# RWKV-7 and band attention on one core: the inverse's products on 64x64 tiles, head sums as float32 products

## The chip, the cores and the metric

The kernel runs on one core of a Trainium2 chip. A core has TensorE (matrix products; in the profile PE for the products and PEld for the loads of their stationary, left operand), VectorE (DVE), ScalarE (ACT), GpSimd (POOL) and SyncE (SP), which work side by side and wait for each other through semaphores; transfers run on 16 DMA engines. SBUF holds operands in 128 partitions, PSUM takes the products. The metric is the time of one execution on the device, in microseconds.

## The reference, cut to what matters

Two layers over 256 tokens of width 2048: first an RWKV-7 layer (time mixing and an MLP), then a layer of chunked band attention (and an MLP), with adaLN modulation everywhere. The change lies in the time mixing, a recurrence over tokens for each of 32 heads of width 64:

```python
def step(S, inp):
    r_t, w_t, k_t, v_t, kk_t, a_t = inp
    sa = jnp.einsum('bhvk,bhk->bhv', S, -kk_t)
    S = (S * w_t[:, :, None, :] + sa[..., None] * (kk_t * a_t)[:, :, None, :]
         + v_t[..., None] * k_t[:, :, None, :])
    y = jnp.einsum('bhvk,bhk->bhv', S, r_t)
    return S, y
```

Three sums over the 64 elements of a head stand around it: the squared length of `kk`, by which `kk` is divided; the sum of `r*k*r_k`, which is multiplied by `v` and added to `y`; and the variance of `y` in the group norm.

## The kernel before, in words

Activations lie transposed: channels in partitions, the 256 tokens along the free side. The 2048 channels are 16 blocks of 128 partitions, and a block holds two heads of 64: a "pair". The large products use a split of each float32 operand into a rounded part and a remainder (`halves`, `split`), and take three single-pass products in two instructions (`proj2`, L394 and L395, tiles `pj`).

The recurrence is computed in chunks of 64 tokens, four chunks for a head. Within a chunk it needs the inverse of a 64x64 unit triangular matrix I + A, where A comes from the products `gr` of L97. `Pair.invert` builds it by doubling: the inverse of the diagonal blocks of size 1 is known; level l joins blocks of 2^l to blocks of 2^(l+1) by two products, with the part of A that couples them (`al`: A times a 0/-1 mask) as left operand of the first. Up to level 4 everything stays inside the two diagonal 32x32 blocks of a head's 64x64 matrix. Level 5 joins those two blocks by the corner block.

In the kernel before, the two diagonal blocks of the two heads of a pair lie under each other: `da` is 128 partitions x 4 chunks x 32, a 32-partition strip (`QS`) per block. The corner blocks lie in `co`. `Pair.tiles` (L103) makes a level's product as 16 small products of 32x32 on four diagonal tiles of TensorE. A level is: a transpose of `u` by VectorE (`tt`, L235), a mask by GpSimd (`al`, L239), a product into `iv`, a copy by ScalarE (`xs`, L241), a second product, an addition by VectorE (L252). Level 0 needs no product (L222, L224). Level 5 works with the strips crosswise, and GpSimd and VectorE put the 64x64 inverse together in `uf` (L247, L256).

A head sum (`head_sums`, L120) is a product with a 128x128 matrix of ones in each head's block (`bones`). It takes single-pass products: `parts` (L110 to L115) lets ScalarE write the rounded values `sH`, and GpSimd the remainder `sL`, and the product is taken of both.

What sets the order: `layer_a` (stages at its end) runs the pairs as a pipeline. In round p, TensorE has the projections of pair p (`proj_steps`, the "dense" work), `early` of pair p-1 (lora products, decay, normalised operands, two head sums), `invert` of pair p-2 and `late` of pair p-3 (the chain over the four chunks, tiles `chn` and `py`, and the third head sum). A round has 16 slots; in each slot `late`, `invert` and `early` advance by their share of steps (a step ends at a `yield`), and then the dense work, held behind the last product of the small work of the slot before. In the last three rounds the first output projections (`out_steps`, L383 to L385, tiles `o`) are the dense work. Within these edges the framework's planner sets the order on each engine. The weights and the adaLN matrix (`acc`, L423) stream in on SyncE's queue all the time.

Of the kernel before, what the change touches and what calls it, by code (L numbers as in the profile page):

```python
# [36 lines left out]
def _constants():  # L37
    i = np.arange(C)
    parts, at = [], {}

    def put(name, a):
        a = np.asarray(a, np.float32)
        if a.shape[0] == C:
            a = np.concatenate([a, a], 0)
        at[name] = (sum(p.shape[1] for p in parts), a.shape[1])
        parts.append(a)

    put("cols", np.tile(np.array([RMS_EPS, GN_EPS, -0.5, 1.0, 1 / 32], np.float32), (P, 1)))
# [12 lines left out]
    p = np.arange(P)  # L61
    bones = (p[:, None] // C == p[None, :] // C).astype(np.float32)
# [7 lines left out]
QS = [slice(H * i, H * i + H) for i in range(4)]  # L70
C_RMS, C_GN, C_MHALF, C_ONE, C_32ND = range(5)


class Pair:
# [15 lines left out]
    @staticmethod  # L90
    def ch(t):
        return t.rearrange("p (c t) -> p c t", t=C)

    def each(self, o, lhsT, rhs):
        for c in range(4):
            for K in self.heads:
                self.b.nc.tensor.matmul(o(c)[K], lhsT(c)[K], rhs(c)[K], start=True, stop=True)  # L97

    def tiles(self, o, lhsT, rhs, pairs):

        for c in range(4):
            for R, K in pairs:
                self.b.nc.tensor.matmul(o[QS[K], c, :], lhsT[QS[R], c, :], rhs[QS[R], c, :], start=True, stop=True,  # L103
                                        tile_position=(H * R, H * K))

    def parts(self, func, src, scale=1.0):

        nc, pw = self.b.nc, self.b.pw
        H, L = (pw.tile([P, T], F32R, tag=n, bufs=2, name=n) for n in ("sH", "sL"))
        nc.scalar.activation(H, src, func, scale=scale)  # L110
        if func != AF.Copy:
            t = self.s("pt", 2)
            nc.scalar.activation(t, src, func, scale=scale)
            src = t
        nc.gpsimd.tensor_tensor(out=L, in0=src, in1=H, op=ALU.subtract)  # L115
        return H, L

    def head_sums(self, ps, parts):
        for i, t in enumerate(parts):
            self.b.nc.tensor.matmul(ps, self.b.bones, t, start=(i == 0), stop=(i == 1))  # L120

    def early(self):
# [7 lines left out]
        nc.tensor.matmul(z[:, 0:T], lw[:, 0, :], self.tw, start=True, stop=True)  # L130
        nc.tensor.matmul(z[:, T:2 * T], lw[:, 1, :], self.ta, start=True, stop=True)
# [7 lines left out]
        sq = self.parts(AF.Square, k, vec("k_k", j))  # L139
# [39 lines left out]
        rkp = self.parts(AF.Copy, rkp)  # L179
# [13 lines left out]
    def invert(self):  # L193
        b, nc, s, ch, kr, bk, bh, kh = self.b, self.b.nc, self.s, self.ch, self.kr, self.bk, self.bh, self.kh
        cst, pp = b.cst, b.pp

        def every(name):
            return cst(name).unsqueeze(1).to_broadcast([P, 4, H])

        def half(name, bufs):  # L200
            return b.pw.tile([P, 4, H], F32, tag=name, bufs=bufs, name=name)

# [28 lines left out]
        uf = self.u = b.uf[self.j % 2]  # L231
        down, up = ((0, 1), (2, 3)), ((1, 0), (3, 2))
        for l in range(1, 6):
            tt_, xs = half("tt", 1), half("xs", 1)
            nc.vector.transpose(out=tt_.rearrange("p c t -> p (c t)"), in_=u.rearrange("p c t -> p (c t)"))  # L235
            pi = pp.tile([P, 16, H], F32, tag="iv", bufs=1, name="iv")[:, 0:4, :]
            if l < 5:
                al = half("al", 2)
                nc.gpsimd.tensor_tensor(out=al, in0=da, in1=every(f"lev{l}"), op=ALU.mult)  # L239
                self.tiles(pi, al, tt_, [(i, i) for i in range(4)])  # L240
                nc.scalar.copy(xs, pi)  # L241
            else:
                self.tiles(pi, co, tt_, down)
                for i, K in enumerate(QS):
                    if i % 2:
                        nc.scalar.copy(xs[K], pi[K])
                    nc.gpsimd.tensor_copy(uf[K, :, H * (i % 2):H * (i % 2) + H], u[K])  # L247
            yield
            pi = pp.tile([P, 16, H], F32, tag="iv", bufs=1, name="iv")[:, 0:4, :]
# [12 lines left out]
            yield  # L262

    def late(self):
# [7 lines left out]
        for c in range(4):  # L272
            pch = pp.tile([P, 3, C], F32, tag="chn", bufs=1, name="chn")
            g, sa = (pw.tile([P, C], F32, tag=n_, bufs=2, name=n_) for n_ in ("g", "sa"))
            for K in heads:
                nc.tensor.matmul(pch[K, 0, :], mk[K, c, 0:C], bk[K, 2, c, :], start=True, stop=(c == 0))  # L276
            if c:
                for K in heads:
                    nc.tensor.matmul(pch[K, 0, :], kr[K, c, 0:C], zs[K, :], start=False, stop=True)
            nc.scalar.copy(g, pch[:, 0, :])  # L280
            yield
            for K in heads:
                nc.tensor.matmul(pch[K, 1, :], u[K, c, :], g[K, :], start=True, stop=True)
            nc.scalar.mul(sa, pch[:, 1, :], -1.0)
            for K in heads:
                nc.tensor.matmul(ch(py)[K, c, :], bk[K, 2, c, :], mk[K, c, C:P], start=True, stop=False)
            if c:
                for K in heads:
                    nc.tensor.matmul(ch(py)[K, c, :], zs[K, :], kr[K, c, C:P], start=False, stop=False)
            yield  # L290
            if c < 3:
                for K in heads:
                    nc.tensor.matmul(pch[K, 2, :], bk[K, 1, c, :], bk[K, 2, c, :], start=True, stop=False)
                for K in heads:
                    nc.tensor.matmul(pch[K, 2, :], bk[K, 0, c, :], sa[K, :], start=False, stop=True)
# [7 lines left out]
            for K in heads:  # L303
                nc.tensor.matmul(ch(py)[K, c, :], sa[K, :], ch(ar)[K, c, :], start=False, stop=True)
# [3 lines left out]
        sq = self.parts(AF.Square, py)  # L308
# [8 lines left out]
        for i in range(2):  # L317
            nc.tensor.matmul(pg, self.lg[:, i, :], self.tg[:, i, :], start=(i == 0), stop=(i == 1))
# [5 lines left out]
class Body:  # L324
# [8 lines left out]
    def cst(self, name, rows=slice(None)):  # L333
        o, n = CST_AT[name]
        return self.csts[rows, o:o + n]
# [184 lines left out]
    def run(self):  # L520
# [16 lines left out]
        self.lazy, self.fins = False, iter(())  # L537
        self.ada_done = set()
# [40 lines left out]
    def layer_a(self, st, sp):  # L579
# [169 lines left out]
        with ExitStack() as s1:  # L749
# [5 lines left out]
            self.bones = pw.tile([P, P], F32R, name="bones")  # L755
            self.uf = [pw.tile([P, 4, C], F32, name=f"uf_{i}") for i in range(2)]
            nc.scalar.copy(self.bones, self.cst("bones"))
            for e, u in zip(e01, self.uf):
                nc.vector.memset(e[:, :, 0:1], 1.0)
                nc.gpsimd.memset(u, 0.0)  # L760
# [39 lines left out]
            stages = ((Pair.late, 16), (Pair.invert, 13), (Pair.early, Pair.EARLY), (None, 16))  # L800
# [290 lines left out]
```

## Time and profile before

| | |
|---|---|
| runs of the kernel before, us | 2772.35, 2776.08, 2783.49 (median 2776.08) |
| the profiled execution's own time, us | 2773.6 |
| its span, us | 2771.8 |
| mean granted TensorE clock | 0.986 |
| 32x32 product instructions (L103) | 4608, from 256.5 to 735.4 us |

The span is the time from the first to the last instruction that the profiler recorded. Each group of instructions has its line in the kernel, the tiles it writes and reads (`out<-in`), its shape (for products the rows and columns of TensorE that it uses, then the moving operand), a count, busy time and mean duration. Matmuls overlap, so the distance between starts says more than a duration. "A <- B" says that A waited for B.

### The profile page before, as it was taken

The numbers are of one execution on the slowest core, as the hardware profiler recorded it, in microseconds if no ns is written. First come the engines' busy times: TensorE is split into PE (matmuls) and PEld (weight loads), VectorE is DVE, ScalarE is ACT, GpSimd is POOL, SyncE is SP. The second block draws the span as 40 slices with busy tenths as digits, with TensorE's granted clock in tenths as the row PEclk, the third lists the DMA queues.
The fourth block names the chain that finished last, engine by engine and source line by source line (L and its number), as shares of the span: only waits on it lengthen the run. The fifth ranks groups of instructions, "written<-read, shape, count | busy, mean of one in ns | idle before, by whom it ended". The sixth has DMA issues, their size and how long they took to land.

```text
span 2771.8 us, 57644 instructions
## 1 busy us (share of the span) xinstructions
PE 2653.9 (96%) x23402; PEld 2217.6 (80%) x23402; DVE 2087.3 (75%) x3098; ACT 1260.9 (45%) x2214; POOL 301.8 (11%) x416
## 2 busy tenths in 40 slices
PE   6998999999998999999999899999989999999997
PEld 3677777777887888888888788877878888888886
DVE  4568778878889888888788896799786566665665
ACT  2345555556344434344344354465444344443444
POOL 0003443443220000000000200000100000000002
PEclk9999999999999999999999999999999999999999
DMA  9886556555687888888888868888876555555553
GB/s 297 269 281 193 169 171 196 176 176 162 216 302 243 298 308 305 300 314 296 299 306 302 304 218 282 268 293 268 279 242 216 187 186 186 187 183 189 185 188 122
DMA packets 217387, 662.60 MB, mean 239 GB/s; under 512 B 21408, under 2 KB 68896, under 8 KB 217120
## 3 DMA queue, kind: packets, MB, share of 16 engines
q1 hardware_dynamic: 215056, 656.36, 71.5%
q8 instruction: 184, 3.01, 0.4%
q10 hardware_dynamic: 2064, 2.54, 0.3%
q14 instruction: 83, 0.68, 0.1%
HBM read 656.72 MB, written 2.10 MB: 238 GB/s over the span
## 4 chain that ended last, share of the span: by engine, by line
PE 76%; DVE 9%; DMA 7%; issue 4%; POOL 1%; ACT 1%; DVEq 0%; SPq 0%; ACTq 0%; POOLq 0%
PE pj L394 40%; PE pj L395 20%; DMA raw<-w_ada 5%; DVE wL L363 3%; DVE acc L423 2%; PE iv L103 2%; PE gr L97 1%; DMA raw<-w_ada_kv 1%; PE m L625 1%; DVE un L504 1%; PE o L383 1%; PE ms L97 1%; POOL sL L115 1%; PE chn L276 1%; DVE aHL L506 1%
## 5 line engine op out<-in xcount | busy, mean ns | idle before, releaser
L394 PE MATMUL pj<-aHL,wH 128*128 128x512 f32 x3712 | 1353.5, 405 | 26.0 <-DVE aHL L506 22.4
L360 ACT CAST wH<-raw 128x1024 fp32r<-128x1024 f32 x772 | 807.0, 1047 | 949.4 <-PE pj L394 622.1
L363 DVE TENSOR_TENSOR wL<-raw,wH 128x1024 fp32r<-128x1024 f32 x772 | 946.1, 1228 | 290.7 <-ACT wH L360 288.8
L395 PE MATMUL pj<-aHL,wL 128*128 128x256 f32 x3712 | 1049.3, 283 | 7.5 <-DVE wL L363 7.2
L394 PEld LDWEIGHTS pj<-aHL,wH 128*128 128x128 f32 x3712 | 700.3, 189 | 199.2 <-issue 28.0
L394 PE MATMUL pj<-hHL,wH 128*128 128x512 f32 x2048 | 722.0, 397 | 4.5 <-DVE hHL L882 4.5
L395 PEld LDWEIGHTS pj<-aHL,wL 128*128 128x128 f32 x3712 | 705.3, 190 | 14.6 <-DVE wL L363 11.9
L395 PE MATMUL pj<-hHL,wL 128*128 128x256 f32 x2048 | 574.3, 281 | 4.6 <-DVE wL L363 4.5
L423 DVE SCALAR_TENSOR_TENSOR acc<-raw,ct,acc 128x1024 f32<-128x1024 f32 x360 | 470.4, 1307 | 139.8 <-DMA raw<-w_ada 104.0
L394 PEld LDWEIGHTS pj<-hHL,wH 128*128 128x128 f32 x2048 | 384.3, 188 | 97.9 <-DVE hHL L882 6.7
L395 PEld LDWEIGHTS pj<-hHL,wL 128*128 128x128 f32 x2048 | 386.8, 189 | 8.1 <-DVE wL L363 7.7
L482 POOL TENSOR_TENSOR ss<-ss,sq 128x256 f32<-128x256 f32 x56 | 65.0, 1160 | 1599.7 <-ACT sq L481 1599.4
L901 DVE SCALAR_TENSOR_TENSOR x<-pj,mod,x 128x256 f32<-128x256 f32 x256 | 123.1, 481 | 51.7 <-PE pj L395 48.8
L881 ACT CAST hHL<-t 128x256 fp32r<-128x256 f32 x128 | 51.4, 403 | 67.6 <-DVE t L880 67.3
L625 PE MATMUL m<-rawa,crep 128*32 128x256 f32 x512 | 47.4, 449 | 17.5 <-DMA rawa<-w_ada 16.9
L481 ACT ACTIVATE sq<-x 128x256 f32<-128x256 f32 x60 | 25.0, 418 | 70.5 <-DVE x L901 39.6
L880 DVE SCALAR_TENSOR_TENSOR t<-t 128x256 f32<-128x256 f32 x128 | 53.9, 422 | 3.0
L882 DVE TENSOR_TENSOR hHL<-t,hHL 128x256 fp32r<-128x256 f32 x128 | 53.4, 418 | 0.6 <-ACT hHL L881 0.5
L862 DVE TENSOR_TENSOR t<-pj,t 128x256 f32<-128x256 f32 x128 | 53.2, 417 | 0.0
L239 POOL TENSOR_TENSOR al<-da,csts 128x128 f32<-128x128 f32 x64 | 40.7, 647 | 67.4 <-PE iv L103 62.7
L861 ACT COPY t<-pj 128x256 f32<-128x256 f32 x128 | 46.6, 366 | 0.0
L685 PE MATMUL t<-aHL,wH 128*128 128x256 f32 x128 | 38.1, 298 | 5.8 <-DVE v L693 3.6
(230 smaller groups left out, 2483.0 us busy)
## 6 DMA issues: line engine op xcount, KB each, us to landing
raw<-w_ada SPq DMA_DIRECT2D x320, 512.0 KB, 4.7
raw<-w_up SPq DMA_DIRECT2D x256, 512.0 KB, 4.9
raw<-w_down SPq DMA_DIRECT2D x256, 512.0 KB, 4.3
rawa<-w_ada SPq DMA_DIRECT2D x64, 512.0 KB, 6.8
raw<-w_ada_kv SPq DMA_DIRECT2D x64, 512.0 KB, 5.4
raw<-w_k SPq DMA_DIRECT2D x32, 512.0 KB, 4.2
raw<-w_r SPq DMA_DIRECT2D x32, 512.0 KB, 4.7
raw<-w_o SPq DMA_DIRECT2D x32, 512.0 KB, 5.2
```

The source lines that it names most:

```text
L97: self.b.nc.tensor.matmul(o(c)[K], lhsT(c)[K], rhs(c)[K], start=True, stop=True)
L103: self.b.nc.tensor.matmul(o[QS[K], c, :], lhsT[QS[R], c, :], rhs[QS[R], c, :], start=True, stop=True, tile_position=(H * R, H * K))
L360: nc.scalar.copy(Hf, raw)
L363: eng.tensor_tensor(out=Lf, in0=raw, in1=Hf, op=ALU.subtract)
L394: nc.tensor.matmul(ps, H[:, i, :], a(kt), start=(kt == 0), stop=False)
L395: ins = nc.tensor.matmul(ps[:, 0, :], L[:, i, :], a(kt)[:, 0, :], start=False, stop=(kt == KT - 1))
L423: nc.vector.scalar_tensor_tensor(out=acc, in0=raw, scalar=ck, in1=acc, op0=ALU.mult, op1=ALU.add)
L482: (eng or nc.gpsimd).tensor_tensor(out=self.ss, in0=self.ss, in1=sq, op=ALU.add)
L625: nc.tensor.matmul(ps[g:g + 32, part, :W], crep[:, kt, :], raw[:, i, :], start=(part == 1 and kt < 4), stop=(part == 0 and kt >= KT - 4), ...
L880: nc.vector.scalar_tensor_tensor(out=t, in0=t, scalar=0.0, in1=t, op0=ALU.max, op1=ALU.mult)
L882: nc.vector.tensor_tensor(out=h[:, 1, :], in0=t, in1=h[:, 0, :], op=ALU.subtract)
L901: nc.vector.scalar_tensor_tensor(out=x, in0=ps[:, i, :], scalar=self.mods[(layer, 5)][:, n:n + 1], in1=x, op0=ALU.mult, op1=ALU.add)
```

## The change

The diagonal blocks are not taken out of A any more: `A` is a copy of the whole 64x64 matrices (128 partitions x 4 chunks x 64), and the level masks are 64 columns wide. A product of the inverse is made by `each` (L97's form): eight products of 64x64, one per chunk and head, whose moving operand `tt` or `u` has 32 columns (a head's two diagonal blocks under each other). For this the left operand must be 64x64 with zeros off the two blocks: the mask sees to it in the first product of a level; for the second, ScalarE copies the first product twice, once with the even strips kept and the odd ones zeroed, once the other way round (`spread`, with the new constant columns `C_EVEN`, `C_ODD`). Level 0 is now a product of its own with the identity, followed by an addition and a transpose. Level 5 uses two tiles that are zeroed once (`corner`), of which only one half is written. `uf` comes from a ring of two tiles.

A head sum is now two float32 products of 64x64 form (one per head, ones as left operand, 256 moving columns) on the unsplit values; `parts`, `sH`, `sL`, `bones` and `QS` are gone. The share of `invert` is 12 steps in 16 slots in place of 13. All matmuls of `Pair` go through a wrapper `mm`, whose flag `in_order` is off.

```diff
-        put(f"lev{l}", np.tile(-m.T[:H, :H].astype(np.float32), (2, 1)))
+        put(f"lev{l}", -m.T.astype(np.float32))
...
-    put("bones", bones)
...
-    def head_sums(self, ps, parts):
-        for i, t in enumerate(parts):
-            self.b.nc.tensor.matmul(ps, self.b.bones, t, start=(i == 0), stop=(i == 1))
+                self.b.mm(o(c)[K], lhsT(c)[K], rhs(c)[K], start=True, stop=True)
+
+    def head_sums(self, ps, t):
+        for K in self.heads:
+            self.b.mm(ps[K], self.b.cst("ones")[K, 0:C], t[K], start=True, stop=True)
...
-        sq = self.parts(AF.Square, k, vec("k_k", j))
+        sq = s()
+        nc.scalar.activation(sq, k, AF.Square, scale=vec("k_k", j))
...
-        rkp = self.parts(AF.Copy, rkp)
...
+        def spread(t):
+            return t.rearrange("p (c i t) -> p c i t", c=4, i=2)
+
+        def level(l):
+            t = s("al", 2)
+            nc.gpsimd.tensor_tensor(out=ch(t), in0=ch(A), in1=cst(f"lev{l}").unsqueeze(1).to_broadcast([P, 4, C]),
+                                    op=ALU.mult)
+            return t
+
+        def product(lhsT, rhs):
+            pi = pp.tile([P, 16, H], F32, tag="iv", bufs=1, name="iv")[:, 0:4, :]
+            self.each(lambda c: pi[:, c, :], lambda c: ch(lhsT)[:, c, :], rhs)
+            return pi
+
+        def turned(t):
+            o = blocks("tt", 1) if t is not tt else blocks("u", 2)
+            nc.vector.transpose(out=o.rearrange("p c t -> p (c t)"), in_=t.rearrange("p c t -> p (c t)"))
+            return o
...
-        da, co, u = half("da", 2), half("co", 2), half("u", 2)
-        for i, K in enumerate(QS):
-            n = H * (i % 2)
-            nc.scalar.copy(da[K], pg[K, :, n:n + H])
-            if i % 2 == 0:
-                nc.scalar.mul(co[K], pg[K, :, H:C], -1.0)
-        nc.gpsimd.tensor_tensor(out=u, in0=da, in1=every("lev0"), op=ALU.mult)
-        yield
-        nc.vector.tensor_tensor(out=u, in0=u, in1=every("eye_h"), op=ALU.add)
+        A = s("da", 2)
+        nc.scalar.copy(ch(A), pg[:, :, 0:C])
+        al = level(0)
+        yield
+        eye_h = cst("eye_h").unsqueeze(1).to_broadcast([P, 4, H])
+        pi = product(al, lambda c: cst("eye_h"))
+        tt = blocks("tt", 1)
+        nc.vector.tensor_tensor(out=tt, in0=pi, in1=eye_h, op=ALU.add)
+        u = turned(tt)
...
             if l < 5:
-                al = half("al", 2)
-                nc.gpsimd.tensor_tensor(out=al, in0=da, in1=every(f"lev{l}"), op=ALU.mult)
-                self.tiles(pi, al, tt_, [(i, i) for i in range(4)])
-                nc.scalar.copy(xs, pi)
+                pi = product(level(l), lambda c: tt[:, c, :])
+                xs = s("xs", 1)
+                for i, own in enumerate((even, odd)):
+                    nc.scalar.activation(spread(xs)[:, :, i, :], pi, AF.Copy, scale=own)
             else:
-                self.tiles(pi, co, tt_, down)
-                for i, K in enumerate(QS):
-                    if i % 2:
-                        nc.scalar.copy(xs[K], pi[K])
-                    nc.gpsimd.tensor_copy(uf[K, :, H * (i % 2):H * (i % 2) + H], u[K])
+                nc.scalar.activation(spread(b.corner[0])[:, :, 1, :], spread(A)[:, :, 1, :], AF.Copy,
+                                     scale=b.col(C_NEVEN))
+                pi = product(b.corner[0], lambda c: tt[:, c, :])
+                xs = b.corner[1]
+                nc.scalar.copy(spread(xs)[:, :, 0, :], pi)
+                nc.scalar.activation(spread(uf)[:, :, 0, :], u, AF.Copy, scale=even)
             yield
+            pi = product(xs, lambda c: u[:, c, :])
             if l < 5:
-                self.tiles(pi, xs, u, [(i, i) for i in range(4)])
                 nc.vector.tensor_tensor(out=u, in0=u, in1=pi, op=ALU.add)
+                tt = turned(u)
             else:
-                self.tiles(pi, xs, u, up)
-                for K in QS[::2]:
-                    nc.vector.tensor_copy(uf[K, :, H:C], pi[K])
+                nc.vector.scalar_tensor_tensor(out=spread(uf)[:, :, 1, :], in0=u, scalar=odd, in1=pi,
+                                               op0=ALU.mult, op1=ALU.add)
...
-        sq = self.parts(AF.Square, py)
+        sq = s("sl", 3)
+        nc.scalar.activation(sq, py, AF.Square)
...
+    def mm(self, *args, **kw):
+        ins = self.nc.tensor.matmul(*args, **kw)
+        return self.tc.keep_in_program_order(ins) if self.in_order else ins
...
-            stages = ((Pair.late, 16), (Pair.invert, 13), (Pair.early, Pair.EARLY), (None, 16))
+            stages = ((Pair.late, 16), (Pair.invert, 12), (Pair.early, Pair.EARLY), (None, 16))
```

More of the change, by code (lines that the diff above doesn't have):

```diff
@@ L46, in put @@
         parts.append(a)
-    put("cols", np.tile(np.array([RMS_EPS, GN_EPS, -0.5, 1.0, 1 / 32], np.float32), (P, 1)))
+    odd = np.arange(P)[:, None] // H % 2
+    put("cols", np.concatenate([np.tile(np.array([RMS_EPS, GN_EPS, -0.5, 1.0, 1 / 32], np.float32), (P, 1)),
+                                1 - odd, odd, odd - 1], 1))
     put("ones", np.ones((P, P)))
@@ L69 @@
 CST, CST_AT = _constants()
-QS = [slice(H * i, H * i + H) for i in range(4)]
-C_RMS, C_GN, C_MHALF, C_ONE, C_32ND = range(5)
+C_RMS, C_GN, C_MHALF, C_ONE, C_32ND, C_EVEN, C_ODD, C_NEVEN = range(8)
 class Pair:
@@ L129, in early @@
         z = b.psm()
-        nc.tensor.matmul(z[:, 0:T], lw[:, 0, :], self.tw, start=True, stop=True)
-        nc.tensor.matmul(z[:, T:2 * T], lw[:, 1, :], self.ta, start=True, stop=True)
+        b.mm(z[:, 0:T], lw[:, 0, :], self.tw, start=True, stop=True)
+        b.mm(z[:, T:2 * T], lw[:, 1, :], self.ta, start=True, stop=True)
         sw, a = s(), s()
@@ L194, in invert, with blocks @@
         b, nc, s, ch, kr, bk, bh, kh = self.b, self.b.nc, self.s, self.ch, self.kr, self.bk, self.bh, self.kh
[L195 to L200, printed above, removed]
+        cst, pp, tt = b.cst, b.pp, None
+        def blocks(name, bufs):
             return b.pw.tile([P, 4, H], F32, tag=name, bufs=bufs, name=name)
+        def spread(t):
[13 more added lines that the diff above has]
+            return o
         ui = cst("ui").unsqueeze(1).to_broadcast([P, 4, P])
@@ L275, in late @@
             for K in heads:
-                nc.tensor.matmul(pch[K, 0, :], mk[K, c, 0:C], bk[K, 2, c, :], start=True, stop=(c == 0))
+                b.mm(pch[K, 0, :], mk[K, c, 0:C], bk[K, 2, c, :], start=True, stop=(c == 0))
             if c:
                 for K in heads:
-                    nc.tensor.matmul(pch[K, 0, :], kr[K, c, 0:C], zs[K, :], start=False, stop=True)
+                    b.mm(pch[K, 0, :], kr[K, c, 0:C], zs[K, :], start=False, stop=True)
             nc.scalar.copy(g, pch[:, 0, :])
@@ L292, in late @@
                 for K in heads:
[L293 removed]
+                    b.mm(pch[K, 2, :], bk[K, 1, c, :], bk[K, 2, c, :], start=True, stop=False)
                 for K in heads:
[L295 removed]
+                    b.mm(pch[K, 2, :], bk[K, 0, c, :], sa[K, :], start=False, stop=True)
                 zn = pw.tile([P, C], F32, tag="zs", bufs=2, name="zs")
@@ L303, in late @@
             for K in heads:
-                nc.tensor.matmul(ch(py)[K, c, :], sa[K, :], ch(ar)[K, c, :], start=False, stop=True)
+                b.mm(ch(py)[K, c, :], sa[K, :], ch(ar)[K, c, :], start=False, stop=True)
             yield
         var, pg = pyt[:, 1, :], pyt[:, 1, :]
-        sq = self.parts(AF.Square, py)
+        sq = s("sl", 3)
+        nc.scalar.activation(sq, py, AF.Square)
         yield
@@ L317, in late @@
         for i in range(2):
-            nc.tensor.matmul(pg, self.lg[:, i, :], self.tg[:, i, :], start=(i == 0), stop=(i == 1))
+            b.mm(pg, self.lg[:, i, :], self.tg[:, i, :], start=(i == 0), stop=(i == 1))
         nc.vector.scalar_tensor_tensor(out=rg, in0=v, scalar=b.vec("ln_b", j), in1=rg, op0=ALU.add, op1=ALU.add)
@@ L754, in layer_a @@
             e01 = [pw.tile([P, 4, C + 1], F32, name=f"e01_{i}") for i in range(2)]
[L755 to L758, printed above, removed]
+            self.corner = [pw.tile([P, T], F32, name=f"corner_{i}") for i in range(2)]
+            for e, u in zip(e01, self.corner):
                 nc.vector.memset(e[:, :, 0:1], 1.0)
```

33 lines of the change are left out of this document (6 added, 27 removed).

## The prediction

> **What bounds the kernel now.** I read the page first, then the busy times of the stretch in which the changed functions run, then what TensorE waits for there, and last the order of time on TensorE, because there the price of one product can be read.
>
> ```profile
> span 2771.8 us, 57644 instructions
> ...
> PE 2653.9 (96%) x23402; PEld 2217.6 (80%) x23402; DVE 2087.3 (75%) x3098; ACT 1260.9 (45%) x2214; POOL 301.8 (11%) x416
> ```
>
> The first and last inverse product of the kernel, and the first and last place where 64x64 work follows one, are these, in order of time on TensorE (start, time to the end of the group's last instruction, line, tile, shape, count):
>
> ```profile
> 256.48 0.45 PE L103 MATMUL iv<-tt,al 32*32 32x32 f32 x32 [1.12 <-DVE tt L235]
> ...
> 289.39 0.32 PE L103 MATMUL iv<-u,xs 32*32 32x32 f32 x14
> 289.64 0.33 PE L276 MATMUL chn<-bk,mk 64*64 64x64 f32 x4
> ...
> 723.22 0.45 PE L103 MATMUL iv<-u,xs 32*32 32x32 f32 x32
> 723.60 0.55 PE L97 MATMUL gr<-kr,kh 64*64 64x128 f32 x6
> ...
> 732.07 0.45 PE L103 MATMUL iv<-u,xs 32*32 32x32 f32 x32
> ```
>
> So everything that the change touches lies between 255 and 740 us; the rest of the span (MLPs, attention) keeps its instructions. The busy times of that stretch, first of all instructions (engines in the order PE, PEld, DVE, ACT, POOL, then clock), then of line 103 alone:
>
> ```profile
> 255.00:740.00 485.00, 470.68 (x9108) 368.52 (x9103) 391.93 (x725) 255.46 (x709) 198.24 (x261) 0.99 0.56 178
> ...
> 255.00:740.00 485.00, 73.98 (x4608) 55.71 (x4608) 0.99 0.56 178
> ```
>
> TensorE is busy for 470.7 of 485 us, at a clock of 0.99. VectorE has 93 us free, ScalarE 230, GpSimd 287. The waits of TensorE between 250 and 760 us (total, times, longest):
>
> ```profile
> PE py L120 <- POOL sL L115: 7.7, 4, 2.2
> PE iv L103 <- DVE tt L235: 4.2, 5, 2.0
> ...
> PE iv L103 <- ACT xs L241: 0.4, 1, 0.4
> ```
>
> These are small, and the largest is a wait for the rounding remainder that the head sums need and that the change removes. So I cost the change as occupancy of TensorE: each us of products added there is a us of time, unless it fills one of these waits.
>
> **The price of one product.** A busy time is not an occupancy, since matmuls are pipelined, so I go by distances from start to start:
>
> ```profile
> 501.57 1.15 PE L97 MATMUL ms<-csts,s 64*64 64x64 f32 x32
> 502.65 0.43 PE L435 MATMUL ms<-csts,acc 128*32 128x1 f32 x32
> 503.01 0.33 PE L293 MATMUL chn<-bk 64*64 64x64 f32 x4
> 503.17 0.28 PE L295 MATMUL chn<-sa,bk 64*64 64x64 f32 x4
> 503.29 0.28 PE L304 MATMUL py<-ar,sa 64*64 64x64 f32 x4
> 503.50 0.45 PE L103 MATMUL iv<-tt,al 32*32 32x32 f32 x32
> 503.89 0.50 PE L394 MATMUL pj<-aHL,wH 128*128 128x512 f32 x1
> ...
> 506.93 0.39 PE L120 MATMUL ms<-sH,bones 128*128 128x256 f32 x1
> 507.15 0.28 PE L120 MATMUL ms<-sL,bones 128*128 128x256 f32 x1
> 507.27 0.40 PE L394 MATMUL pj<-aHL,wH 128*128 128x512 f32 x1
> ...
> 508.06 0.45 PE L103 MATMUL iv<-tt,al 32*32 32x32 f32 x32
> 508.44 0.33 PE L293 MATMUL chn<-bk 64*64 64x64 f32 x4
> ...
> 510.76 1.09 PE L97 MATMUL gr<-kr,kh 64*64 64x128 f32 x16
> 511.78 0.50 PE L394 MATMUL pj<-aHL,wH 128*128 128x512 f32 x1
> ```
>
> A float32 matmul is recorded as two instructions: the 16 small products of a level show as x32, the eight products of a 64x64 call as x16. And these rows say how long a weight load and a matmul take (shortest, median, longest in ns):
>
> ```profile
> L103 PEld LDWEIGHTS iv<-u,xs x2304: 101/108/153, 257.6 to 735.3; 32*32 32x32 f32 x192
> L103 PE MATMUL iv<-u,xs x2304: 191/191/258, 257.6 to 735.4; 32*32 32x32 f32 x192
> ...
> L97 PEld LDWEIGHTS ms<-csts,s x512: 129/135/135, 250.0 to 713.9; 64*64 64x64 f32 x171
> ...
> L394 PEld LDWEIGHTS pj<-aHL,wH x3712: 186/188/334, 221.7 to 2665.1; 128*128 128x128 f32 x196
> ```
>
> *32x32 today.* The group at 503.50 is busy 0.45 us; without the 0.191 of its last matmul, 0.26 us lie between its first and last start. Its 32 instructions run as 8 rounds over four tiles, so a round is 0.26/8 = 0.032 us. *64x64 with 64 moving columns.* The four instructions at 503.17 take 0.12 us to the next start: two rounds over two tiles, 0.058 each. The group at 501.57 agrees: 16 rounds in 1.08 us with its entry and exit.
>
> *64x64 with 32 moving columns*, which the change makes, stands nowhere in the trace. Bounds: 0.032 a round if the moving columns set it, 0.058 if the 64 columns of the weight load do. I take 0.058. The loads take 108, 135 and 188 ns for 32, 64 and 128 columns, so each 32 columns more cost 27 ns whatever is streamed; and the group at 502.65, with one moving column and a 32-column load, needs 0.36/8 = 0.045 us a round with entry and exit, hardly less than the product at 503.50 with 32 moving columns and the same load (0.39/8 = 0.049). So 32 moving columns don't set the round; the load does, or a fixed floor, which is the first rival.
>
> **The change part by part.**
>
> *Products.* Before: 16 pairs x 10 products x 8 rounds x 0.032 = 41 us. After: one product more per pair (the first level now goes through TensorE), 16 x 11 x 8 x 0.058 = 82 us. Level 5 loses nothing today by having half the tiles (its 16 instructions are 8 rounds of two), so it counts in full on both sides. Difference +41 us; with the low price of a round 45 - 41 = +4.
>
> *Entries and exits.* Changing from 64x64 to 32x32 costs: the four instructions at 503.29 need 0.21 us to the next start where those at 503.17 need 0.12, so 0.09. By the list of all starts 92 products stand right behind 64x64 work (first 256.48, last 732.07): -8 us. Leaving towards 64x64 work costs 0.38 - 0.26 = 0.12 us at 508.06 where a plain next round is 0.058, and the first round after it is dearer by its exposed load (0.17 at 503.01 against 0.12), 0.11 together; 42 such places (289.39 to 723.22): -5. Products that stay between dense work pay a larger first load, some 0.04 us, 66 times: +3. Sum -10; if the order of work keeps none of these neighbours, 0.
>
> *Head sums.* Before, two matmuls over all rows: 0.34 us at 506.93 with their entry, 0.12 the second, so 0.24 inside. After, four instructions with 256 moving columns in 64x64 form, two heads side by side. No row has it. The group at 510.76 has 128 columns: 16 instructions in 1.02 us, less entry and exit about 0.107 a round; twice that is 0.214, two rounds 0.43. If the heads did not overlap it would be 0.86, and it can't be below the 0.24 of the single-pass form. I take 0.43: 48 sums x 0.19 = +9 us (0 to +30).
>
> *The wait that goes.* The 7.7 us before the sum of squares of y wait on GpSimd. This place costs more than the wait:
>
> ```profile
> 364.86 0.28 PE L120 MATMUL py<-sH,bones 128*128 128x256 f32 x1
> 367.23 0.39 PE L120 MATMUL py<-sL,bones 128*128 128x256 f32 x1 [2.09 <-POOL sL L115]
> ...
> 369.39 1.85 PE L97 MATMUL gr<-kr,bh 64*64 64x128 f32 x14
> ```
>
> After a gap of 2.09 us the next matmuls run slowly: 14 instructions in 1.85 us where 16 took 1.09. That is at least 0.9 us; four waits give some 4 us. After the change the sum waits for one ScalarE square, about 0.4 us, and dense products lie between. So -12 us. On this the Trainium skill, "TensorE: Matmul & The Clock Gate", section "Why this matters for your kernels", says to avoid idle gaps over about 3 us, or the clock halves; the row shows slow matmuls after 2.09 us already. By the page the 4 us would not go and the sum would be 4 higher.
>
> *The other engines.* Rows of the groups on GpSimd and ScalarE (busy, mean ns):
>
> ```profile
> L239 POOL TENSOR_TENSOR al<-da,csts 128x128 f32<-128x128 f32 x64 | 40.7, 647 | 67.4 <-PE iv L103 62.7 <-PE chn L279 4.7
> L247 POOL COPY uf<-u 32x128 f32<-32x128 f32 x64 | 33.1, 517 | 2.5
> L115 POOL TENSOR_TENSOR sL<-pt,sH 128x256 fp32r<-128x256 f32 x32 | 32.6, 1018 | 48.5 <-ACT pt L113 24.2 <-PE o L384 19.0 <-ACT sH L110 3.9
> L208 POOL TENSOR_TENSOR s<-kh,pc 128x256 f32<-128x256 f32 x16 | 20.6, 1284 | 2.5 <-DVE kh L178 2.5
> ...
> L241 ACT COPY xs<-iv 128x128 f32<-128x128 f32 x64 | 16.9, 264 | 33.0 <-PE iv L103 32.7
> ```
>
> GpSimd's level masks double in size: five of at most 1.28 us (the L208 row of that size), 6.4 us a pair, against 4 x 0.65 + 4 x 0.52 + 3 x 1.02 = 7.7 that go. ScalarE copies each first product twice, 0.264 us more per level, and drops six small copies and three rounding passes a pair. VectorE keeps its additions and transposes. None of this ends last: they stand beside the dense products, and ScalarE alone has 230 us free. What could show is the first product, which now waits for copy and mask: if each pair waited as the 1.12 us at 256.48, 18 us; I take 0, since a step comes every 2.2 us (485 us over 18 rounds of 12 steps) and the mask is no longer behind six copies. The pace of 12 steps in 16 slots in place of 13, the 35 more constant columns and the new zeroed tiles move nothing on TensorE: 0. The wrapper around matmul passes each on unchanged while its flag is off: 0.
>
> *Sum.* +41 - 10 + 9 - 12 = +28; the other waits between 250 and 740 (485 - 470.7 = 14, less the 7.7) shrink when VectorE and the loads get more time, some 3: +25. The profiled execution's span is 2771.8 us, its own time is 2773.6; +25 gives 2799. The median of the runs is 2.5 us above it, so 2801.
>
> **The rivals.**
>
> *A fixed floor sets the round.* Then a round of the new products costs 0.032 as well, since it streams no more columns than today's: +4 in place of +41, and +25 becomes -12, 2764 us. For it speaks that the one-column round at 502.65 and the 32-column one at 503.50 are alike; against it that the load's time grows by 27 ns per 32 columns. The Trainium skill, "TensorEngine Tiling (Array Packing)", section "Instruction Overhead", has such a floor: a matmul of one column lasts as long as one of 60. No row here shows a 64-column load with fewer than 64 moving columns, which alone would tell.
>
> *The inverse's own chain becomes the bound.* TensorE takes its work in order, so a product not ready holds the dense ones behind it. One more copy per level (0.264 x 5 x 16 = 21 us) and 1.12 us at each first product (18 us) give 2801 + 39 = 2840. It decides once a level's chain is longer than the slot between its steps. For it: the wait at 256.48. Against it: 0.4 us of waits for this copy in the whole stretch.
>
> *The other side: the added products are hidden.* If TensorE's busy 97% hides room and the stretch is really paced by GpSimd and VectorE, the 41 + 9 us vanish in it and what is left is the removed wait: -12 and the 4.2 us on the transpose, 2776 - 16 = 2760. It decides once more than 30 of the 50 us fit into gaps. Against it: from 503.01 to 503.89 each start follows the last at the round's price, and all waits listed make up under 15 us.
>
> **How the numbers follow.** The forecast (weight load sets the round) has 0.74, its own range 2785 to 2820. The fixed floor has 0.10, the chain 0.11, the hidden products 0.05. Half a per cent, about what a measurement of this kernel can tell from no change, is 14 us: 2762 and 2790. The forecast's low end (0.08) and the fixed floor give "same" 0.18, the hidden products "faster" 0.05, the rest is slower, 0.77. The range leaves out the hidden products, the fixed floor and the chain's upper part: 2768 to 2830.
>
> **What would show it.** In the changed kernel the products at 64*64 32x32 show as 2816 instructions (x16 each), about 0.46 us from start to the next start, with weight loads near 135 ns; no gap between 64x64 neighbours and them; head sums of four instructions in 0.43 us; no wait on sL; and a stretch of about 510 us in place of 485, with the rest unmoved. Wrong would be: x16 in 0.26 us, new waits of products for xs or al in the tens of us, or a stretch that keeps its length.

## The result, and the profile after

The changed kernel took 2797.51 us (median of 4 runs, 2795.16 to 2801.63) against 2779.53 us for the kernel before in the same session. The ratio is 1.0069, with a 95% interval of 1.0042 to 1.0097: slower by 0.7%, 18 us between the medians. The profiled execution of the changed kernel has a span of 2794.3 us, 22.5 more than before.

The page of the changed kernel, its head and the row of engines:

```profile
span 2794.3 us, 54126 instructions
...
PE 2693.1 (96%) x21706; PEld 2244.7 (80%) x21706; DVE 2078.7 (74%) x3082; ACT 1256.6 (45%) x2165; POOL 239.8 (9%) x304
```

There are 1696 matmuls fewer, and TensorE is busy 39 us longer. GpSimd has 62 us less to do. The difference lies in one stage, from the first projection of the first pair to the last head sum of y. Its two ends can be read from the first and last starts of these rows, first of the kernel before, then of the changed one:

```profile
L394 PEld LDWEIGHTS pj<-aHL,wH x3712: 186/188/334, 221.7 to 2665.1; 128*128 128x128 f32 x196
...
L120 PE MATMUL py<-sL,bones x16: 274/282/388, 304.2 to 755.7; 128*128 128x256 f32 x16
```

```profile
L392 PEld LDWEIGHTS pj<-aHL,wH x3712: 186/188/331, 217.1 to 2688.0; 128*128 128x128 f32 x196
...
L340 PE MATMUL py<-sl,csts x64: 376/402/427, 295.8 to 780.0; 64*64 64x256 f32 x64
```

The stage took 755.7 - 221.7 = 534.0 us before and 780.0 - 217.1 = 562.9 after, so 28.9 more. The changed kernel entered it 4.6 us earlier and needed 2 us less behind it. The medians of the runs differ by 18 us only, so some 10 of the 28.9 belong to these two executions or are won back outside the stage; which of the two is not shown. The stage is still the better place to read causes: what comes behind it took 2010 to 2027 us in the kernels of this study, although none of them changed an instruction there, and one execution of the same kernel differs from another by several us. Part of that is the clock: 23 runs of the kernel before in one session lay between 2769 and 2788 us, and the 10 of them with a mean granted clock of 0.985 or less took 5 us more on average than the other 13.

The products of the inverse in the changed kernel, loads and matmuls in ns, and the order of time on TensorE around one of them and around a sum of y:

```profile
L340 PEld LDWEIGHTS iv<-u,xs x1024: 129/135/135, 251.2 to 757.8; 64*64 64x64 f32 x171
L340 PE MATMUL iv<-u,xs x1024: 189/219/240, 251.2 to 757.9; 64*64 64x32 f32 x171
```

```profile
516.36 0.66 PE L340 MATMUL iv<-u,xs 64*64 64x32 f32 x16
516.95 0.50 PE L392 MATMUL pj<-aHL,wH 128*128 128x512 f32 x1
...
519.16 0.28 PE L340 MATMUL py<-ar,sa 64*64 64x64 f32 x4
519.28 0.61 PE L340 MATMUL iv<-tt,al 64*64 64x32 f32 x16
519.82 0.50 PE L392 MATMUL pj<-aHL,wH 128*128 128x512 f32 x1
...
524.16 0.66 PE L340 MATMUL iv<-tt,al 64*64 64x32 f32 x16
524.64 0.31 PE L340 MATMUL py<-ar,sa 64*64 64x64 f32 x4
...
527.31 0.40 PE L392 MATMUL pj<-aHL,wH 128*128 128x512 f32 x1
527.54 0.28 PE L393 MATMUL pj<-aHL,wL 128*128 128x256 f32 x1
527.75 0.65 PE L340 MATMUL py<-sl,csts 64*64 64x256 f32 x4
528.33 0.50 PE L392 MATMUL pj<-aHL,wH 128*128 128x512 f32 x1
528.66 0.28 PE L393 MATMUL pj<-aHL,wL 128*128 128x256 f32 x1
```

The product at 519.28 follows 64x64 work after 0.12 us, without an entry. It is busy 0.61 us; without the 0.219 of its last matmul 0.39 us lie between its first and last start, seven rounds of 0.056. With its exit it holds TensorE 0.54 us, where a product on 32x32 tiles held it 0.38 to 0.39. The one at 516.36 stands between dense products and holds TensorE 0.59 us, the one at 524.16 has dense work before it and 64x64 work behind it and holds it 0.48.

The waits of TensorE between 250 and 790 us in the changed kernel:

```profile
PE iv L340 <- POOL al L185: 5.9, 6, 1.5
PE o L381 <- ACT aHL L515: 1.3, 1, 1.3
PE iv L340 <- DVE tt L196: 0.2, 1, 0.2
```

The wait on the remainder is gone, and the one on the transpose is down to 0.2 us. A new one stands in their place: the first product of a pair waits for GpSimd's mask.

From the list of all matmul starts I added up the time from each start to the next, by the kind of instruction that starts it:

| us in the stage | before | after | difference |
|---|---|---|---|
| products of the inverse (`iv`) | 65.9 | 95.7 | +29.8 |
| head sums, with the waits between their two matmuls | 25.0 | 26.5 | +1.5 |
| other 64x64 work | 150.0 | 140.5 | -9.5 |
| dense products (`pj`, `o`) | 262.3 | 272.3 | +10.0 |
| the rest | 30.9 | 27.9 | -3.0 |

The dense products are the same 1270 instructions in both. What differs is how often they are interrupted: 240 times before and 288 times after, a dense instruction is followed by one of another tile form. A dense instruction of 256 moving columns takes 0.120 us to the next start, and 0.214 if a smaller form follows; the one behind a group of smaller form takes some 0.1 more as well. So 48 more interruptions at 0.09 + 0.10 are 9 of the 10 us.

### The profile page after: what moved, and what is told of

It is laid out like the page before. It is cut to its first block, busy times and chain, and to the rows that moved or that the text cites. A ratio compares the mean times of both kernels' runs of the same rounds, so it can differ in the third digit from the quotient of the medians.

```text
span 2794.3 us, 54126 instructions
## 1 busy us (share of the span) xinstructions
PE 2693.1 (96%) x21706; PEld 2244.7 (80%) x21706; DVE 2078.7 (74%) x3082; ACT 1256.6 (45%) x2165; POOL 239.8 (9%) x304
## 4 chain that ended last, share of the span: by engine, by line
PE 75%; DVE 5%; DMA 4%; issue 4%; POOL 1%; ACT 0%; DVEq 0%; SPq 0%; POOLq 0%; ACTq 0%
PE pj L392 43%; PE pj L393 21%; DMA raw<-w_ada 4%; PE iv L340 3%; DVE wL L361 2%; PE chn L340 2%; PE ms L340 1%; PE py L340 1%; DVE acc L421 1%; PE gr L340 1%; DMA raw<-w_ada_kv 1%; PE o L381 1%; POOL s L204 0%; PE o L382 0%; PE o L383 0%
## 5 line engine op out<-in xcount | busy, mean ns | idle before, releaser
L185 POOL TENSOR_TENSOR al<-da,csts 128x256 f32<-128x256 f32 x80 | 78.6, 991 | 245.0 <-ACT da L213 157.3
L234 ACT ACTIVATE xs<-iv,csts 128x128 f32<-128x128 f32 x128 | 40.1, 365 | 51.8 <-PE iv L340 51.3
L624 PE MATMUL m<-rawa,crep 128*32 128x256 f32 x512 | 46.4, 440 | 16.8 <-DMA rawa<-w_ada 16.3
L245 DVE TENSOR_TENSOR u<-u,iv 128x128 f32<-128x128 f32 x64 | 18.2, 284 | 41.8 <-PE iv L340 41.6
```

The source lines that it names most:

```text
L185: nc.gpsimd.tensor_tensor(out=ch(t), in0=ch(A), in1=cst(f"lev{l}").unsqueeze(1).to_broadcast([P, 4, C]), op=ALU.mult)
```

## The experiments

The stage is measured in each kernel as above. "Before" is the kernel before, run beside each.

| kernel | ratio to before, 95% interval | stage, us | of it at clock 0.5, us |
|---|---|---|---|
| before | 1 | 534.0 | 10.2 |
| changed | 1.0069 [1.0042, 1.0097] | 562.9 | 6.8 |
| head sums only | 1.0023 [1.0007, 1.0040] | 536.9 | 0 |
| products only | 1.0056 [1.0036, 1.0077] | 554.3 | 0 |
| changed, products twice | 1.0401 [1.0376, 1.0425] | 643.4 | 13.7 |
| before, remainder for y on VectorE | 0.9967 [0.9955, 0.9979] | 526.2 | 6.8 |
| changed, 32 columns a load | 1.0047 [1.0031, 1.0064] | 549.9 | 0 |
| changed, longer chain | 1.0088 [1.0068, 1.0108] | 564.6 | 0 |
| before, float32 sum for y only | 1.0005 [0.9991, 1.0019] | 531.6 | 3.4 |
| before, products twice | 1.0297 [1.0272, 1.0322] | 609.3 | 30.7 |
| before, remainder on VectorE, early transpose | 0.9957 [0.9944, 0.9970] | 523.6 | 3.4 |

The last column is the time within the stage in which the granted TensorE clock of the profiled execution was 0.5 and not 1. Half of it is an estimate of what that cost, so the stages of two kernels that differ by less than some 5 us (15 for the doubled small products) can differ by the clock of the one execution alone. "At equal clock" means below that half of this column is taken off each stage: 528.9 us are left for the kernel before and 559.5 for the changed one.

### The two halves of the change

The kernel before with the new head sums alone:

```diff
-    def head_sums(self, ps, parts):
-        for i, t in enumerate(parts):
-            self.b.nc.tensor.matmul(ps, self.b.bones, t, start=(i == 0), stop=(i == 1))
+    def head_sums(self, ps, t):
+        for K in self.heads:
+            self.b.nc.tensor.matmul(ps[K], self.b.cst("ones")[K, 0:C], t[K], start=True, stop=True)
...
-        sq = self.parts(AF.Square, k, vec("k_k", j))
+        sq = s()
+        nc.scalar.activation(sq, k, AF.Square, scale=vec("k_k", j))
```

> The kernel before with the head sums alone changed to float32 products on 64x64 tiles; the inverse stays on 32x32 tiles. By my sum: 48 sums cost 0.19 us more each (+9), the wait of the sum of squares of y on the remainder and the slow matmuls after it go (-12): 3 us less than before, within -8 to +2. If the head sums are what makes the changed kernel slower, +10 to +20. In the trace no wait on sL, and sums of four instructions in about 0.43 us.

Measured: ratio 1.0023, 6 us slower, and 2.9 us more in the stage (8 at equal clock). My sum had 3 us less. The waits on `sL` are gone. The price of a sum in its rows is as I had it: at 531.02 us in this kernel one sum stands behind other 64x64 work and gives way to dense work.

```profile
530.91 0.28 PE L289 MATMUL py<-kr,zs 64*64 64x64 f32 x4
531.02 0.60 PE L120 MATMUL ms<-s,csts 64*64 64x256 f32 x4
531.55 0.50 PE L395 MATMUL pj<-aHL,wH 128*128 128x512 f32 x1
```

That is 0.53 us with an exit of some 0.1. What I had left out is the interruption. In the kernel before, a sum between dense products cost no change of form, as this place of it shows:

```profile
734.43 0.28 PE L385 MATMUL o<-aHL,wL 128*128 128x256 f32 x1
734.54 0.28 PE L120 MATMUL py<-sH,bones 128*128 128x256 f32 x1
734.66 0.28 PE L120 MATMUL py<-sL,bones 128*128 128x256 f32 x1
734.78 0.29 PE L383 MATMUL o<-aHL,wH 128*128 128x256 f32 x1
```

Four starts at even distances, 0.24 us for the sum and no gap on either side. As 64x64 products the sums break the dense work 41 times more (281 against 240), and the dense products take 6.7 us more.

The changed kernel with the head sums of before:

```diff
-        sq = s()
-        nc.scalar.activation(sq, k, AF.Square, scale=vec("k_k", j))
+        sq = self.parts(AF.Square, k, vec("k_k", j))
...
-    def s(self, name="s", bufs=10):
+    def s(self, name="s", bufs=9):
```

> The changed kernel with the head sums of before (rounded part and remainder, 128x128); two rings of tiles are one tile shorter, to make room. By my sum the products alone cost +41 - 10 - 3 = +28 us over before; the two halves should add up to the whole, so this should stand some 3 us above the changed kernel. If the products cost little and the sums much, it stands at before's time. The wait on sL is back: 5 to 10 us.

Measured: ratio 1.0056, 16 us over before, 20.3 in the stage; below my 28, and some 4 us below the changed kernel where I had 3 above, though the two intervals overlap. The wait on `sL` is back with 6 us. In the stage the two halves add to 23.2 of the 28.9, and at equal clock to 33 of 31, so no loss is left that only both together make. Most of the loss is the products, which is what the forecast rested on; the smaller part is the head sums, which I had counted, with the wait that they remove, as a small gain. The dense products of this kernel are interrupted 24 times more than before (264 against 240) and take 6.4 us more, so a part of their growth comes with the products.

### What a product costs

Each product of the changed kernel twice, and each product of the kernel before twice:

```diff
-            self.each(lambda c: pi[:, c, :], lambda c: ch(lhsT)[:, c, :], rhs)
+            for _ in range(2):
+                self.each(lambda c: pi[:, c, :], lambda c: ch(lhsT)[:, c, :], rhs)
...
-        for c in range(4):
-            for R, K in pairs:
...
+        for _ in range(2):
+            for c in range(4):
+                for R, K in pairs:
```

> The changed kernel with every product of the inverse issued twice into the same tile, so 176 more products. If TensorE's order of work is the bound and a round lasts what the weight load does, 176 x 8 x 0.058 = +82 us over the changed kernel, all of it in the stage of the pairs. If the stage has room, because other engines pace it, +40 or less. If the inverse's chain is the bound, more than 82, since the copies wait for the second product too.

Measured: 2887.54 us, 643.4 - 562.9 = 80.5 us more in the stage; 176 products at 0.457 us. That is the 82 of the rounds (77 at equal clock), and nearly all of it arrives: the stage hides next to nothing of TensorE's work, and the chain adds nothing that shows. The whole rose by some 90 us over the changed kernel, 10 more than the stage; what made the rest is not shown. The rival of the hidden products falls here.

> The kernel before with every 32x32 product of the inverse issued twice into the same tile: 160 products more. At 8 rounds of 0.032 us each, +41 us over before; with the 64x64 products doubled it was +90 over the changed kernel for 176 of them. If a 32x32 product costs more of TensorE's time than its rounds show (drains inside the group), +60 or more; if the stage has room, under 25.

Measured: 75.3 us more in the stage, not 41. The order of time on TensorE around a doubled product, and TensorE's longest waits in this kernel:

```profile
517.22 0.28 PE L305 MATMUL py<-ar,sa 64*64 64x64 f32 x4
517.43 0.75 PE L104 MATMUL iv<-u,xs 32*32 32x32 f32 x64
518.11 0.50 PE L395 MATMUL pj<-aHL,wH 128*128 128x512 f32 x1
```

```profile
PE iv L104 <- issue: 14.7, 17, 2.1
PE iv L104 <- DVE tt L236: 4.9, 8, 1.1
PE pj L395 <- issue: 2.8, 2, 2.0
```

The doubled group holds TensorE for 0.68 us where the single one held it 0.38, so the second product costs 0.30 and not 0.26: 48 us for 160. By the list of starts only the second is slower: the first 32 instructions of a doubled group start within 0.262 us, as those of a single group in the kernel before, the second 32 within 0.288. Another 14.7 us are gaps, most of them in the middle of products, in which nothing that the profile shows was missing; I read them as TensorE waiting for its instructions, of which the small products need the most for their work (9216 matmuls here), but no run tests that. The remaining 12 us lie in the dense products. Some 5.5 of these are longer gaps behind a dense product (6.5 us against 1.0), and an estimated 6 are the clock: 16.3 us of the dense products' time fall into stretches at clock 0.5 (the longest from 561.0 to 574.6), against 4.3 before. So the doubled kernel is no measure of a product that stands alone, whose rounds stay at the 0.032 us that I had taken.

### What sets a round

The changed kernel, each product cut into two of 64 rows and 32 columns:

```diff
-            self.each(lambda c: pi[:, c, :], lambda c: ch(lhsT)[:, c, :], rhs)
+            for c in range(4):
+                for i in range(2):
+                    for K in self.heads:
+                        n = K.start + H * i
+                        b.nc.tensor.matmul(pi[n:n + H, c, :], ch(lhsT)[K, c, H * i:H * i + H], rhs(c)[K],
+                                           start=True, stop=True, tile_position=(K.start, n))
```

> The changed kernel, with each 64x64 product of the inverse cut into two of 64 rows and 32 columns, side by side on the array: the same operands and the same 32 moving columns, twice the instructions, half the columns in a weight load. If the columns of the load set the round, a round falls from 0.058 to 0.032 us for four instructions and the products cost 176 x 8 x 0.026 = 37 us less; the change of the tile form against the 64x64 neighbours comes back (up to +20), so 15 to 37 us less than the changed kernel, and the weight loads of the products take about 108 ns in place of 135. If the 64 rows or the 64x64 form set the round, a product keeps 0.46 us or gets longer: 0 to +40.

```profile
L195 PEld LDWEIGHTS iv<-tt,al x2048: 102/110/111, 249.1 to 742.4; 64*32 64x32 f32 x187
```

```profile
517.82 0.45 PE L195 MATMUL iv<-tt,al 64*32 64x32 f32 x32
518.20 0.39 PE L398 MATMUL pj<-aHL,wL 128*128 128x256 f32 x1
518.52 0.33 PE L345 MATMUL py<-ar,sa 64*64 64x64 f32 x4
```

The same operands, rows and moving columns, twice the instructions, and a product holds TensorE 0.38 us in place of 0.54: the columns of the load set the round, not the moving side and not the rows. The floor of the first rival is out. The stage got only 13 us shorter (10 at equal clock) and the whole some 6, where I had expected 15 to 37: the products fell from 95.7 to 69.4 us, but the other 64x64 work rose from 140.5 to 153.8, since it changes form against the products again. The Trainium skill, "TensorE: Matmul & The Clock Gate", section "LDWEIGHTS (loading the stationary operand)", gives P/1.2 ns for a load of P columns; by an estimate from it, 64 columns take 53 ns and 32 take 27. Rounds of 0.058 and 0.032 us are that and 5 ns in both cases, so the trace agrees.

### Is the chain near to being the bound?

In the changed kernel, one of the two copies of a first product is made twice:

```diff
                     nc.scalar.activation(spread(xs)[:, :, i, :], pi, AF.Copy, scale=own)
+                    if i == 0:
+                        nc.scalar.activation(spread(xs)[:, :, i, :], pi, AF.Copy, scale=own)
```

> The changed kernel with one of the two ScalarE copies of each first product made twice, so that every level's chain is 0.37 us longer while TensorE's own work stays the same. If TensorE's occupancy is the bound, 0 to +4 us over the changed kernel. If the inverse's chain is the bound, 64 levels x 0.37 = +24.

Measured: the stage 1.7 us longer (5 at equal clock), ratio 1.0088, 5 us more than the changed kernel, with an interval that overlaps its interval widely. In the waits of this kernel the copy hardly appears:

```profile
PE iv L342 <- POOL al L185: 3.0, 4, 1.0
...
PE iv L342 <- ACT xs L234: 0.2, 1, 0.2
```

So of the 24 us that a chain as the bound would cost at most 5 are there: the chain has room for most of 0.37 us a level, and the second rival is out.

### What the wait on GpSimd was worth

The kernel before, with only the remainder for the sum of y on VectorE:

```diff
-        sq = self.parts(AF.Square, py)
+        sq = self.parts(AF.Square, py, eng=nc.vector)
```

> The kernel before, with the remainder for the sum of squares of y taken by VectorE in place of GpSimd. If the waits on sL before line 120 and the slow matmuls behind them are worth 12 us, 8 to 12 us less than before, since VectorE takes 0.42 us for it and has time. If the wait only moves (VectorE is late too, behind a product of 1.3 us), 0 to -4.

```profile
PE iv L103 <- DVE tt L235: 4.7, 5, 2.0
PE o L385 <- DVE wL L363: 3.7, 1, 3.7
PE ms L120 <- POOL sL L115: 1.3, 2, 1.0
```

Measured: ratio 0.9967, 9 us faster than before, 7.8 of it in the stage. The wait is gone, and no other took its place: the 3.7 us before `o` lie behind the stage, where the kernel before has 3.3 on the same line. Its worth is 6 us (at equal clock) to 9 rather than my 12.

The kernel before, with a float32 sum for y alone:

```diff
-        sq = self.parts(AF.Square, py)
+        sq = s("sl", 3)
+        nc.scalar.activation(sq, py, AF.Square)
         yield
-        self.head_sums(var, sq)
+        self.head_sums32(var, sq)
```

> The kernel before, with only the sum of squares of y as float32 products; the other two sums keep the split. After the run with all three sums changed (6 us slower where I had 3 faster) I reckon that a 64x64 sum between dense products also pays an entry and an exit, some 0.28 us, so 0.47 each. For the 16 sums of y that is +7.5, the wait of 7.7 and the slow matmuls behind it go (-12): 2 to 7 us less than before. If the price of the sums is something else, bound to all three alike, this is no faster than before.

Measured: ratio 1.0005, the same as before; in the stage 2.4 us less, which is the clock (1 us more at equal clock, as in the whole). Both this kernel and the one with the remainder on VectorE lose the same wait; with the float32 sum the stage is 531.6 - 526.2 = 5.4 us longer than with the split one (7 at equal clock), 0.34 us for each of 16 sums. The other 32 sums cost 536.9 - 531.6 = 5.3 more (also 7), 0.17 each. The neighbours explain a part of this difference: by the list of starts a float32 sum between dense products holds TensorE 0.58 us and a split one 0.24, but with 64x64 work before them and dense work behind 0.53 and 0.34. They do not explain all of it, since with all sums in float32 14 of those 32 stand between dense products too.

### A version faster than both

The transposes placed right behind each update of `u`, as the changed kernel has them, in the kernel with the remainder on VectorE:

```diff
+        tt_ = turned()
...
                 nc.vector.tensor_tensor(out=u, in0=u, in1=pi, op=ALU.add)
+                tt_ = turned()
```

> The kernel with 32x32 products and the remainder for y on VectorE, and beside it the transpose of u right behind each update of u, as the changed kernel has it, in place of at the start of the next level. The waits of the products on that transpose (4.2 us before, 4.7 us with the remainder on VectorE; 0.2 us in the changed kernel) should go: 3 to 5 us less than with the remainder on VectorE alone, so 11 to 16 us less than before. If the planner had placed the transpose as early as it could anyway, no difference to the version without.

```profile
PE iv L103 <- DVE tt L228: 4.6, 5, 2.0
```

Measured: ratio 0.9957, 12 us faster than before, but its interval holds most of that of the version without the early transpose, its stage is only 1 us shorter than there at equal clock, and the wait on the transpose stands as it was. So the place of the transpose in the code does not make this wait; what does is open. The remainder on VectorE is what beats both kernels.

## Why the prediction was right, point by point

The forecast was 2801 us and slower; 2797.5 were measured. The mechanism, more occupancy of TensorE in a stage that has next to nothing to hide it, was right: doubling the products costs nearly their full price, and a longer chain costs little. The sum of +25 stands against +22.5 in the span and +18 between the medians. That it came so near is luck in part: the products were taken some 11 us too dear, and the dense work, which got 10 us longer, had no term at all.

- *Products, +41.* By the list of starts the products grew by 30 us. The rounds were right on both sides: by the same list 0.032 us from round to round in a single old product, and 0.457 us for the eight of a second new one, where I had 0.464. What was mis-sized is the rest of the time that a product holds TensorE. An old one held it some 0.38 us whatever stood beside it, 0.13 over its rounds; a new one 0.59 between dense products, which is about as much over, but 0.54 or 0.48 with 64x64 work on one side and, by the list, 0.44 with it on both.
- *Entries and exits, -10.* The other 64x64 work got 9.5 us shorter, as it no longer changes form against the products; the gain at the products themselves, above, comes on top of that. In the kernel with half the columns that gain goes away again, 13 us.
- *Head sums, +9.* The inside of a sum was right (0.43 us and an exit), and without the waits (8.3 us before) the sums grew by some 10 us. The step that failed is that they cost only this. The old sums had the form of the dense products beside them; the new ones interrupt these. With the new first product of each pair the dense work is broken 48 times more, 10 us that no term had.
- *The wait that goes, -12.* It went, and was worth 6 to 9. I had slow matmuls behind all four waits; they follow two of them. The waits ended at 304.2, 367.2, 429.8 and 616.4 us after 1.95, 2.09, 1.47 and 2.19 us, and the granted clock of the kernel before (third from the end of each row, which has the busy times of a stretch of 50 us) is below 1 only behind the second and the last:

```profile
300.00:350.00 50.00, 47.69 (x878) 37.25 (x870) 36.84 (x70) 28.20 (x78) 23.72 (x31) 1.00 0.49 155
350.00:400.00 50.00, 47.91 (x919) 36.88 (x920) 40.88 (x75) 24.03 (x68) 20.83 (x27) 0.97 0.61 193
400.00:450.00 50.00, 48.53 (x896) 37.98 (x896) 39.47 (x75) 26.93 (x76) 17.42 (x27) 1.00 0.54 167
...
600.00:650.00 50.00, 47.81 (x912) 36.82 (x911) 40.86 (x78) 24.87 (x69) 21.25 (x28) 0.97 0.60 190
```

  With the remainder on VectorE the clock stays at 1 behind both places; its only time at 0.5 in the stage begins at 264.2, where the kernel before has some too.

- *The other engines, 0.* I named the first product's wait on copy and mask and took 0 of up to 18. It is there: 5.9 us, six times, the longest 1.5.
- *The rest unmoved.* No instruction changed there, but its length varies by several us from one profiled execution to another. The stage grew to 563 us by its landmarks, 29 more; I had it grow by 25.
- *What would show it.* 2816 instructions of x16, loads of 135 ns and no gap against 64x64 neighbours are there. The 0.46 us from start to next start are there only where 64x64 work follows; dense work follows after 0.54 to 0.59.

## What to carry to other kernels

Where TensorE is the bound, as here, price small products by the distance between starts and by what stands beside them, not by their busy time: a left operand padded with zeros cost its full columns in the weight load here, though only 32 columns were streamed past it. Keep products that stand among dense ones in the form of the dense ones, since each interruption cost about 0.2 us here, for the way into the small form and back. And look for the wait first: moving one subtraction to an engine with time gained 9 us, more than the form of all head sums cost.

## What the hardware showed that I had not expected

- A 32x32 product alone takes 0.032 us a round, but the second of two in a row took 0.30 us and not 0.26, and 14.7 us of gaps without a visible cause appeared in the stage. Many tiny instructions had a price that a short group did not show.
- Behind a 2.09 us wait of TensorE the matmuls ran slowly (14 in 1.85 us in place of 16 in 1.09), in the row shown in the prediction: from 367.6 us on the granted clock was 0.5 for 3.4 us. The length of the wait alone did not decide it. In the kernel before no such stretch followed a wait of 1.95 us (304.2), and in the changed kernel one did begin at 373.4, some 1 us after a wait of 1.53 (372.2).
- What lies behind the stage has the same instructions and took 2010 to 2027 us from one kernel to another. A stage is less blurred than the whole, but its time at the lower clock has to be looked at before a difference of 5 us is read from it.
